# Moving weight sums and product splits from GpSimd to VectorE, their DMAs to ScalarE's queue, and decay differences to ScalarE

## The chip, the cores and the metric

One NeuronCore of one Trainium2 chip. The metric is device time in microseconds of one execution of the whole program. The engines are named PE (TensorE, with PEld for its weight loads), DVE (VectorE), ACT (ScalarE), POOL (GpSimd) and SP (SyncE, which here only issues DMAs). Each engine works through its own instructions in order.

## What is computed

Two residual layers over 272 tokens (16 learned meta tokens and 256 frames) of width 2048, all in float32. Layer 0 runs gated linear attention (GLA, 4 heads) beside stick-breaking attention (8 heads); layer 1 is a Mamba-2 mixer (SSD) with 8 groups of 8 heads.

```python
# layer 0
proj = einsum('btd,de->bte', h, w_in)
o_gla = rms_norm_groups(gla(gq, gk, gv, log_a)) * silu(gr)
o_sb  = stick_breaking(sq, sk, sv) * silu(sr)
h = layer_norm(alpha * h + einsum('bte,ed->btd', concat(o_gla, o_sb), w_out))
# layer 1
z, xbc, dt = split(einsum('btd,de->bte', h, w_in)); xbc = silu(conv(xbc))
a_cum = cumsum(dt * a_neg)
l_mat = exp(where(causal, a_cum[t] - a_cum[s], -inf))
y = einsum(l_mat * (C_t . B_s), x * dt) + d_skip * x        # per head
h = layer_norm(alpha * h + einsum('bte,ed->btd', rms_norm_groups(y * silu(z)), w_out))
```

The weights are drawn in float32, and the output is 256 x 2048.

## The kernel before

**Every product in three parts.** The matrix products are made from a high part and a low part of each operand: `three` issues high x high, high x low and low x high (L214 to L216). So each weight tile of 128 x 2048, a *unit*, is loaded on SP's queue (`load_unit`, L176) and split: ScalarE copies it to the rounded type (`whi`, L191), and VectorE subtracts that from the original (`wlo`, L192). `split` takes the engine of the subtraction as an argument. A unit's next-but-one is loaded when it starts, and the next is split while it is multiplied. The unit's 48 matmuls are issued in four quarters of 12.

**Side tasks.** Everything else is written as generators; `tick` advances each running one by one `yield`, once after every quarter of a unit. So a `yield` in a task is a distance of 12 matmuls in the order in which the program is written. The framework's planner then fixes each engine's order from that program order and a simulated timeline.

**Weight sums** (`quad_sums`, layer 0). The output product of layer 1 is made for six of its eight groups (`NS7`) with seven block products in place of eight, which needs sums of blocks of the output weights. For each of 6 groups and 2 column halves, two tiles of 128 x 2048 (four blocks of 512 columns, tile `quad`, one buffer) are loaded, four blocks are replaced by differences in four instructions (L573), and the tile is stored to DRAM (`qs`). These 24 blocks are made during layer 0. Loads (L569) and stores (L577) are on SP's queue, the differences on GpSimd. The steps of one block are 5 yields after the load, 4 differences with a yield each, 2 yields, the store, 2 yields.

**GLA and stick-breaking heads** (layer 0). `mix_gla` and `mix_sb` copy the scores from PSUM to `spad` (ScalarE, L828 and L931), mask them with three selects on GpSimd (`causal`, L288), split them (`parts_of`: ScalarE L680, VectorE L681) and multiply with the values (`values`, L739). TensorE's order has the values at a fixed place between matmuls of the units.

**Block products** (layer 1). `product_load` fetches 128 x 2 x 512 blocks (`praw`, L590), from the weights or from `qs`, on SP's queue; `product_split` splits them, with the subtraction of the 48 that come from `qs` on GpSimd and of the other 36 on VectorE; `product` makes six matmuls (L614) and adds the bank to the accumulator on VectorE (L619). Two loads run ahead.

**Decay** (`decay1`, layer 1). For a group, `load_decay` broadcasts 8 rows of cumulated decays to all partitions (tile `ebc`, one buffer, SP's queue, L1206). For each head VectorE makes min(ebc - est, 0) in two instructions (256 columns, L1239; 144 columns, L1240), `est` being a value per partition; ScalarE takes Exp of two heads at a time (L1242). Later VectorE multiplies with the masked scores `cb` (L1267, four instructions a group), and `mix_ssd` multiplies the result `M` on TensorE (L1424).

GpSimd also has, in layer 1, every third second half of the late units' splits (L192 with `raw`, 21 of them), the gate products and the sums of squares.

Of the kernel before, what the change touches and what calls it, by code (L numbers as in the profile page):

```python
# [8 lines left out]
AF = mybir.ActivationFunctionType  # L9
ALU = mybir.AluOpType  # L10
# [23 lines left out]
def _plan():  # L34
# [36 lines left out]
SEVEN = (  # L71
    ("a11", 0, False, 0, True, (0, 0)),
    ("a12", 3, False, 1, True, (0, 0)),
    ("s2", 2, True, 0, False, (1, 0)),
    ("s3", 1, True, 1, True, (1, 1)),
    ("s1", 0, True, 0, False, (1, 1)),
    ("n22", 3, True, 1, False, (1, 0)),
    ("s4", 2, False, 0, False, (0, 1)),
)
PRODUCTS = [(g, q, n) for g in range(NS7) for q in range(2) for n in range(7)]  # L80
# [19 lines left out]
def _wait(*tasks):  # L100
    for t in tasks:
        while not t.done:
            yield
# [14 lines left out]
class _Body:  # L118
# [440 lines left out]

    def quad_sums(self):  # L560

        nc, sub = self.nc, self.nc.gpsimd.tensor_tensor
        for g in range(NS7):
            for q in range(2):
                d = self.sums[g, q] = self.tc.dram_tile([2, P, 2048], F32, name=self.nm("qs"))
                for c in range(2):
                    b = self.lp.tile([P, 4, 512], F32, tag="quad", name=self.nm("quad"))
                    flat = b.rearrange("p a c -> p (a c)")
                    nc.sync.dma_start(flat, self.quad_rows(g, q)[c])  # L569
                    for _ in range(5):  # L570
                        yield
                    for o, x, y in ((0, 1, 0), (1, 2, 1), (2, 2, 0), (3, 2, 3)):
                        sub(b[:, o, :], b[:, x, :], b[:, y, :], op=ALU.subtract)  # L573
                        yield
                    for _ in range(2):
                        yield
                    nc.sync.dma_start(d[c], flat)  # L577
                    for _ in range(2):
                        yield

    def product_load(self, k):
# [10 lines left out]
    def product_split(self, k):  # L592
        if k >= len(PRODUCTS):
            return
        is_sum = SEVEN[PRODUCTS[k][2]][2]
        raw = self.praw.pop(k).rearrange("p k c -> p (k c)")
        self.pparts[k] = self.split(raw, 1024, self.nc.gpsimd if is_sum else self.nc.vector)

    def product(self, k):

# [612 lines left out]
    def decay1(self, g):  # L1213
        nc, lp = self.nc, self.lp
        act, vec, mm = nc.scalar.activation, nc.vector, nc.tensor.matmul
        bc = self.cur["bc", g]
        self.silu1(bc, None if g else vec)
        yield
        if g:
            yield from _wait(*self.mixers[6 + g - 1])  # L1220
        else:
            yield from _wait(self.tasks["dt"], self.tasks["res"])
            self.load_decay(0)
            yield
            yield
        if g > 1:
            bch, bcl = [a for a in lp.tile([P, 2, T + S], F32R, tag="gz", name=self.nm("bcp")).rearrange("p a c -> a p c")]
            act(bch, bc, AF.Copy)
            vec.tensor_tensor(bcl, bc, bch.bitcast(F32), op=ALU.subtract)
            pairs = ((bch, bch), (bch, bcl), (bcl, bch))  # L1230
        else:
            pairs = ((bc, bc),)

        M = lp.tile([P, HPG, 400], F32, tag="M", name=self.nm("M"))
        self.cur["M", g] = M
        eb = self.cur["ebc", g]
        for h in range(HPG):
            gh = g * HPG + h
            vec.tensor_scalar(M[:, h, 0:256], eb[:, h, 0:256], self.est[:, 0, 0, gh : gh + 1], 0.0, op0=ALU.subtract, op1=ALU.min)  # L1239
            vec.tensor_scalar(M[:, h, 256:400], eb[:, h, 256:400], self.est[:, 0, 1, gh : gh + 1], 0.0, op0=ALU.subtract, op1=ALU.min)  # L1240
            if h % 2:
                act(M[:, h - 1 : h + 1, :], M[:, h - 1 : h + 1, :], AF.Exp)  # L1242
                yield
        mt = self.mt
        e2 = self.est2[:, 0, g * HPG : (g + 1) * HPG].rearrange("p (h o) -> p h o", o=1).broadcast_to([16, HPG, 16])
        vec.tensor_tensor(mt, eb[:16, :, 400:416], e2, op=ALU.subtract)
        vec.tensor_scalar(mt, mt, 0.0, None, op0=ALU.min)
        act(mt, mt, AF.Exp)
        yield

        for _ in range(2 if g else 0):
            yield
        zb = self.zbank()
        pin = self.tc.keep_in_program_order
        for o, s0, n, t0 in ((zb[:, 16:272], 0, P, 0), (zb[:, 272:416], P, P, 112), (zb[:16, 0:16], 2 * P, NM, 240)):
            for i, (b, c) in enumerate(pairs):
                pin(mm(o, b[:, s0 : s0 + n], c[:, T + t0 :], start=i == 0, stop=i == len(pairs) - 1))
        yield
        cb = lp.tile([P, 416], F32, tag="cb", name=self.nm("cb"))
        act(cb, zb[:, :416], AF.Copy)  # L1260
        self.causal(cb[:, 16:128], 112, False, 16)
        self.causal(cb[:, 272:400], 128, False)
        self.causal(cb[:16, 0:16], 16, False)
        yield
        for h in range(0, HPG, 2):
            c = cb[:, 16:416].rearrange("p (o c) -> p o c", o=1).broadcast_to([P, 2, 400])
            vec.tensor_tensor(M[:, h : h + 2, :], M[:, h : h + 2, :], c, op=ALU.mult)  # L1267
            yield
        c = cb[:16, 0:16].rearrange("p (o c) -> p o c", o=1).broadcast_to([16, 2, 16])
        m = mt.rearrange("s (p j i) t -> s j p i t", j=2, i=2)  # L1270
        for j in range(2):
            for p in range(2):
                vec.tensor_tensor(self.mt2[32 * j : 32 * j + 16, 2 * p : 2 * p + 2, j, :], m[:, j, p], c, op=ALU.mult)
        yield
# [391 lines left out]
```

## Time and profile before

| | |
|---|---|
| median of 3 runs | 1528.98 us (1519.80 to 1532.24) |
| the profiled execution | 1524.72 us, span 1522.9 us |
| TensorE busy | 1401.1 us (92%), 10559 matmuls |
| VectorE busy | 1183.1 us (78%) |
| ScalarE busy | 800.3 us (53%) |
| GpSimd busy | 556.3 us (37%) |
| mean granted TensorE clock | 0.960 |
| DMA | 325.96 MB, 214 GB/s |

Layer 0 runs to about 770 us of the span, layer 1 from about 800. In a row of the profile stand the line, the engine, the operation and the tiles written and read (out<-in); a wait names the releaser, and the clock is that granted to TensorE as a share of full speed. A mean length is one over instructions that may have been held up; the minimum or the median of a group shows what the same instruction takes undisturbed.

### The profile page before, as it was taken

How to read it: one execution, taken by the hardware profiler on the slowest of the kernel's cores; microseconds unless marked ns; L12 is line 12 of the kernel's file. 1: busy time of each engine (PE TensorE's matmuls, PEld its weight loads, DVE VectorE, ACT ScalarE, POOL GpSimd, SP SyncE). 2: the span in 40 equal slices, each digit the busy share in tenths (PEclk: the TensorE clock that was granted, in tenths of full speed). 3: DMA queues.
4: the chain of work that ended last, by engine and by line, in shares of the span. 5: the costliest groups of instructions: out<-in, count | busy, mean ns of one | idle time of the engine just before them, and what ended most of it. 6: DMA issues, size and time to landing. Idle time of an engine off the chain costs nothing.

```text
span 1522.9 us, 26579 instructions
## 1 busy us (share of the span) xinstructions
PE 1401.1 (92%) x10559; PEld 1340.8 (88%) x10559; DVE 1183.1 (78%) x1812; ACT 800.3 (53%) x1171; POOL 556.3 (37%) x413
## 2 busy tenths in 40 slices
PE   9899999799899999999949998797987988989998
PEld 8799999799898999999948987797987888889886
DVE  7869676587475664668886998789798987888977
ACT  6446354255254544546765656465564565645661
POOL 2253523433434100017001535454454463545331
PEclk9999999899899999999979999898998999989999
DMA  9878778687676555553445556565665565655551
GB/s 343 289 270 295 276 254 302 248 286 274 233 293 252 168 164 182 176 161 132 166 145 208 201 180 238 167 218 179 229 208 178 196 215 192 214 181 208 185 201 56
DMA packets 88252, 325.96 MB, mean 214 GB/s; under 512 B 27904, under 2 KB 30784, under 8 KB 56640
## 3 DMA queue, kind: packets, MB, share of 16 engines
q1 hardware_dynamic: 87408, 323.48, 60.5%
q8 instruction: 83, 1.36, 0.4%
q10 hardware_dynamic: 720, 0.79, 0.1%
q14 instruction: 41, 0.34, 0.1%
HBM read 293.33 MB, written 30.91 MB: 213 GB/s over the span
## 4 chain that ended last, share of the span: by engine, by line
PE 50%; DVE 18%; DMA 13%; issue 6%; POOL 6%; ACT 4%; SPq 1%; ACTq 0%; POOLq 0%; DVEq 0%
PE pj L214 14%; PE pj L216 14%; PE pj L215 14%; DVE wlo L192 4%; POOL quad L573 4%; DMA quad<-in_wts 4%; PE pj L614 3%; DMA praw<-qs 3%; ACT whi L191 2%; DVE M L1267 2%; DMA qs<-quad 2%; DMA vdr<-vt 2%; DVE M L1239 2%; DMA vt<-vdr 1%; PE po L739 1%
## 5 line engine op out<-in xcount | busy, mean ns | idle before, releaser
L214 PE MATMUL pj<-xhi,whi 128*128 128x272 f32 (+4 forms) x2560 | 742.2, 290 | 29.2 <-DVE xt L1184 12.3
L216 PE MATMUL pj<-xhi,wlo 128*128 128x272 f32 (+4 forms) x2560 | 737.7, 289 | 8.9 <-DVE wlo L192 8.9
L215 PE MATMUL pj<-xlo,whi 128*128 128x272 f32 (+4 forms) x2560 | 738.3, 289 | 0.0
L192 DVE TENSOR_TENSOR wlo<-raw,whi 128x1024 fp32r<-128x1024 f32 (+2 forms) x365 | 502.9, 1385 | 134.6 <-ACT whi L191 132.3
L191 ACT ACTIVATE whi<-raw 128x1024 fp32r<-128x1024 f32 (+2 forms) x386 | 395.9, 1033 | 270.6 <-PE pj L215 206.2
L214 PEld LDWEIGHTS pj<-xhi,whi 128*128 128x128 f32 x2560 | 489.9, 192 | 39.7 <-DVE xt L1184 13.5
L216 PEld LDWEIGHTS pj<-xhi,wlo 128*128 128x128 f32 x2560 | 490.2, 192 | 10.0 <-DVE wlo L192 9.8
L215 PEld LDWEIGHTS pj<-xlo,whi 128*128 128x128 f32 x2560 | 490.0, 191 | 3.5
L573 POOL TENSOR_TENSOR quad<-quad 128x512 f32<-128x512 f32 x96 | 154.1, 1605 | 256.0 <-DMA quad<-in_wts 222.2
L192 POOL TENSOR_TENSOR wlo<-praw,whi 128x1024 fp32r<-128x1024 f32 x48 | 125.8, 2623 | 125.5 <-ACT whi L191 112.7
L191 ACT ACTIVATE whi<-praw 128x1024 fp32r<-128x1024 f32 x84 | 88.4, 1053 | 89.1 <-PE pj L614 41.3
L216 PE MATMUL pj<-mixh,wlo 128*128 128x272 f32 x384 | 112.7, 294 | 0.0
L214 PE MATMUL pj<-mixh,whi 128*128 128x272 f32 x384 | 112.5, 294 | 0.0
L215 PE MATMUL pj<-mixl,whi 128*128 128x272 f32 x384 | 112.4, 293 | 0.0
L1195 POOL TENSOR_TENSOR gz<-gz,xcl 128x512 f32<-128x512 f32 x16 | 28.8, 1801 | 165.6 <-ACT xcl L1194 165.6
L215 PEld LDWEIGHTS pj<-mixl,whi 128*128 128x128 f32 x384 | 74.3, 193 | 0.2
L216 PEld LDWEIGHTS pj<-mixh,wlo 128*128 128x128 f32 x384 | 74.5, 194 | 0.0
L214 PEld LDWEIGHTS pj<-mixh,whi 128*128 128x128 f32 x384 | 74.1, 194 | 0.1
L192 POOL TENSOR_TENSOR wlo<-raw,whi 128x1024 fp32r<-128x1024 f32 x21 | 55.0, 2617 | 47.5 <-ACT whi L191 47.4
L614 PE MATMUL pj<-whi,ssh 128*128 128x512 f32 x96 | 41.5, 432 | 27.8 <-DVE acc L619 25.5
L619 DVE TENSOR_TENSOR acc<-acc,pj 128x512 f32<-128x512 f32 x84 | 56.8, 677 | 12.5 <-PE pj L614 12.2
L1192 ACT ACTIVATE xcl<-xcl 128x544 f32<-128x544 f32 (+2 forms) x40 | 25.5, 639 | 60.0 <-DVE xcl L1191 60.0
(397 smaller groups left out, 1920.1 us busy)
## 6 DMA issues: line engine op xcount, KB each, us to landing
raw<-in_wts SPq DMA_DIRECT2D x188, 1024.0 KB, 6.1
quad<-in_wts SPq DMA_DIRECT2D x24, 1024.0 KB, 6.0
qs<-quad SPq DMA_DIRECT2D x24, 1024.0 KB, 4.8
praw<-qs SPq DMA_DIRECT2D x48, 512.0 KB, 4.4
praw<-in_wts SPq DMA_DIRECT2D x36, 512.0 KB, 4.2
ebc<-edr SPq DMA_DIRECT2D x8, 1664.0 KB, 6.7
raw<-in_wts SPq DMA_DIRECT2D x9, 256.0 KB, 5.5
vdr<-vt SPq DMA_DIRECT2D x8, 256.0 KB, 4.5
```

Source lines behind the costliest of these rows:

```text
L191: self.nc.scalar.activation(hi, src, AF.Copy)
L192: eng.tensor_tensor(lo, src, hi.bitcast(F32), op=ALU.subtract)
L214: mm(ps, whi, xhi, start=first, stop=False)
L215: mm(ps, whi, xlo, start=False, stop=False)
L216: mm(ps, wlo, xhi, start=False, stop=last)
L573: sub(b[:, o, :], b[:, x, :], b[:, y, :], op=ALU.subtract)
L614: mm(ps, a[:, j, :], b[:, j, :], start=f, stop=(j == 1 and a is yl), skip_group_check=True)
L619: self.nc.vector.tensor_tensor(a, a, ps, op=ALU.add)
L1192: act(c, c, AF.Exp, scale=-1.0)
L1195: (eng or self.nc.gpsimd).tensor_tensor(v, v, c, op=ALU.mult)
L1239: vec.tensor_scalar(M[:, h, 0:256], eb[:, h, 0:256], self.est[:, 0, 0, gh : gh + 1], 0.0, op0=ALU.subtract, op1=ALU.min)
L1267: vec.tensor_tensor(M[:, h : h + 2, :], M[:, h : h + 2, :], c, op=ALU.mult)
```

## The change

Four edits. The weight sums' subtractions go from GpSimd to VectorE. Their loads and stores go from SP's queue to ScalarE's, and two more yields stand between a store and the next load. The subtraction of every product split is on VectorE. The decay differences are made on ScalarE: Relu(est - ebc) in place of min(ebc - est, 0), followed by Exp with scale -1.

```diff
     def quad_sums(self):
-        nc, sub = self.nc, self.nc.gpsimd.tensor_tensor
+        nc, sub = self.nc, self.nc.vector.tensor_tensor
...
-                    nc.sync.dma_start(flat, self.quad_rows(g, q)[c])
+                    nc.scalar.dma_start(flat, self.quad_rows(g, q)[c])
                     for _ in range(5):
                         yield
...
-                    nc.sync.dma_start(d[c], flat)
-                    for _ in range(2):
+                    nc.scalar.dma_start(d[c], flat)
+                    for _ in range(4):
                         yield
...
     def product_split(self, k):
-        is_sum = SEVEN[PRODUCTS[k][2]][2]
         raw = self.praw.pop(k).rearrange("p k c -> p (k c)")
-        self.pparts[k] = self.split(raw, 1024, self.nc.gpsimd if is_sum else self.nc.vector)
+        self.pparts[k] = self.split(raw, 1024)
...
-            vec.tensor_scalar(M[:, h, 0:256], eb[:, h, 0:256], self.est[:, 0, 0, gh : gh + 1], 0.0, op0=ALU.subtract, op1=ALU.min)
-            vec.tensor_scalar(M[:, h, 256:400], eb[:, h, 256:400], self.est[:, 0, 1, gh : gh + 1], 0.0, op0=ALU.subtract, op1=ALU.min)
+            for s, c in ((0, slice(0, 256)), (1, slice(256, 400))):
+                act(M[:, h, c], eb[:, h, c], AF.Relu, bias=self.est[:, 0, s, gh : gh + 1], scale=-1.0)
             if h % 2:
-                act(M[:, h - 1 : h + 1, :], M[:, h - 1 : h + 1, :], AF.Exp)
+                act(M[:, h - 1 : h + 1, :], M[:, h - 1 : h + 1, :], AF.Exp, scale=-1.0)
```

## The prediction

> **What bounds the kernel now.** I first read the stages as a table of busy time (columns: stretch and its length, then busy time and instructions of TensorE, its weight loads, VectorE, ScalarE and GpSimd, then granted clock, DMA share, GB/s).
>
> ```profile
> span 1522.9 us, 26579 instructions
> 15.00:500.00 485.00, 454.53 (x3592) 449.64 (x3590) 344.96 (x518) 223.62 (x320) 191.54 (x134) 0.96 0.76 276
> 500.00:770.00 270.00, 268.17 (x2159) 266.48 (x2157) 188.55 (x330) 150.61 (x255) 44.65 (x67) 1.00 0.48 162
> 800.00:1400.00 600.00, 543.61 (x3955) 504.64 (x3954) 511.74 (x704) 340.00 (x466) 277.68 (x174) 0.95 0.58 201
> ```
>
> TensorE is the bound: from 500 to 770 us it is never idle and nothing can be won there. What can be lost or won is its idle time and its slow clock: 30 us idle before 500 us, 56 us idle in the steady part of layer 1, where the clock of 0.95 costs up to another 0.05 x 600 = 30 us. VectorE is the second engine there, busy 85% of the time; ScalarE has 57%.
>
> Second, the waits (who waited for whom, total us, times, longest us), and the timeline at the largest idle stretch of layer 0 (start, length, engine, line).
>
> ```profile
> POOL quad L573 <- DMA quad<-in_wts: 222.2, 20, 24.3
> PE pj L614 <- DVE acc L619: 25.5, 11, 7.9
> ACT s0h L680 <- POOL spad L288: 23.6, 4, 9.6
> 278.27 0.53 ACT L828 ACTIVATE spad<-z 128x432 f32<-128x432 f32 x1 [4.05 <-PE z L825]
> 285.92 5.28 POOL L573 TENSOR_TENSOR quad<-quad 128x512 f32<-128x512 f32 x4 [11.72 <-DMA quad<-in_wts]
> 291.15 0.68 POOL L288 TENSOR_SCALAR_AFFINE_SELECT spad<-spad 128x128 f32<-128x128 f32 x3
> 292.48 0.59 PE L739 MATMUL po<-s0h,gvh 128*128 128x272 f32 x1 [8.49 <-ACT s0h L680]
> ```
>
> The scores of a GLA head are in `spad` at 278.8. GpSimd has only 0.68 us to do on them, the causal selects, but its next instruction in order is a weight-sum subtraction that waits for its DMA until 285.9. So the selects run at 291.15, and TensorE stands for 8.49 us. The next head's stop has the same shape:
>
> ```profile
> 399.44 1.26 POOL L573 TENSOR_TENSOR quad<-quad 128x512 f32<-128x512 f32 x1 [9.93 <-DMA quad<-in_wts]
> 400.66 0.68 POOL L288 TENSOR_SCALAR_AFFINE_SELECT spad<-spad 128x128 f32<-128x128 f32 x3
> 267.00:305.00 38.00, 29.12 (x209) 28.35 (x208) 21.76 (x31) 10.84 (x14) 17.04 (x15) 0.87 0.65 249
> 381.00:419.00 38.00, 31.42 (x219) 30.86 (x218) 18.94 (x30) 10.04 (x14) 17.74 (x14) 0.82 0.64 233
> ```
>
> In these two stretches TensorE is idle 8.9 and 6.6 us and then runs slow: 0.13 x 38 = 4.9 and 0.18 x 38 = 6.8 us at most. Together 27 us.
>
> Third, layer 1, at one of its largest stops:
>
> ```profile
> 953.38 10.68 DVE L1267 TENSOR_TENSOR M<-M,cb 128x800 f32<-128x800 f32 x4 [0.42 <-POOL cb L288]
> 953.46 2.40 POOL L192 TENSOR_TENSOR wlo<-raw,whi 128x1024 fp32r<-128x1024 f32 x1
> 955.83 4.67 POOL L192 TENSOR_TENSOR wlo<-praw,whi 128x1024 fp32r<-128x1024 f32 x2
> 964.59 0.69 DVE L619 TENSOR_TENSOR acc<-acc,pj 128x512 f32<-128x512 f32 x1
> 965.42 0.76 PE L614 MATMUL pj<-whi,ssh 128*128 128x512 f32 x1 [7.67 <-DVE acc L619]
> L1267 DVE TENSOR_TENSOR M<-M,cb 128x800 f32<-128x800 f32 x32 | 51.0, 1651 | 2.7 <-POOL cb L288 2.7
> L1267 DVE TENSOR_TENSOR M<-M,cb x32: 977/984/7976, 815.1 to 1436.5; 128x800 f32<-128x800 f32 x32
> ```
>
> The last two rows are the group (busy us, mean ns) and min/median/max of one. Four products of 0.98 us take 10.68 us, because one lasts 7.98 us: as long as GpSimd runs three splits without a pause (953.46 to 960.50). The accumulation L619 that frees the next product's bank stands behind them, and TensorE waits 7.67 us. VectorE is not only full here, it is held up by GpSimd.
>
> **The change part by part.** Rows for the prices (group rows: busy us, mean ns; tile rows: min/median/max ns):
>
> ```profile
> L573 POOL TENSOR_TENSOR quad<-quad 128x512 f32<-128x512 f32 x96 | 154.1, 1605 | 256.0 <-DMA quad<-in_wts 222.2 <-DMA vt<-vdr 28.5
> L573 POOL TENSOR_TENSOR quad<-quad x96: 1258/1359/2382, 27.1 to 483.0; 128x512 f32<-128x512 f32 x96
> L192 DVE TENSOR_TENSOR wlo<-raw,whi 128x512 fp32r<-128x512 f32 x9 | 6.1, 692 | 0.9 <-ACT whi L191 0.9
> L192 POOL TENSOR_TENSOR wlo<-praw,whi 128x1024 fp32r<-128x1024 f32 x45 | 117.6, 2616 | 119.6 <-ACT whi L191 106.7 <-PE pj L614 10.6 <-DVE wlo L192 2.2
> L192 DVE TENSOR_TENSOR wlo<-praw,whi x36: 1205/1222/1998, 787.7 to 1421.9; 128x1024 fp32r<-128x1024 f32 x36
> L192 DVE TENSOR_TENSOR wlo<-raw,whi 128x1024 fp32r<-128x1024 f32 x109 | 161.4, 1482 | 29.0 <-ACT whi L191 28.1 <-issue 0.4
> L1239 DVE TENSOR_SCALAR M<-ebc,est 128x256 f32<-128x256 f32 x52 | 34.8, 668 | 3.8 <-PE po L1424 3.8
> L1240 DVE TENSOR_SCALAR M<-ebc,est 128x144 f32<-128x144 f32 x52 | 26.1, 503 | 0.0
> L647 ACT ACTIVATE ga<-po,cpk 128x272 f32<-128x272 f32 x8 | 3.8, 480 | 4.7 <-PE po L646 4.7
> L1442 ACT ACTIVATE ys<-y 128x256 f32<-128x256 f32 x24 | 9.6, 402 | 0.0
> L191 ACT ACTIVATE whi<-praw 128x1024 fp32r<-128x1024 f32 x84 | 88.4, 1053 | 89.1 <-PE pj L614 41.3 <-DMA praw<-qs 26.4 <-PE pj L215 9.0
> ACT whi L191 <- PE pj L215: 215.2, 160, 3.2
> 0.84 1.36 ACTq L321 DMA_DIRECT2D raw<-in_wts  x3
> SPq L577 <- POOL quad L573: 99.8, 19, 9.9
> SPq L569 <- DMA qs<-quad: 60.6, 16, 8.1
> SPq L1206 <- DVE M L1240: 69.4, 6, 12.1
> quad<-in_wts SPq DMA_DIRECT2D x24, 1024.0 KB, 6.0
> qs<-quad SPq DMA_DIRECT2D x24, 1024.0 KB, 4.8
> ```
>
> *Weight sums (layer 0).* GpSimd loses 96 x 1.605 = 154 us. VectorE gains 96 x 0.692 = 66 us, in a layer where it is busy 71%. It gets some back: 96 times it no longer shares time with a subtraction. TensorE sees neither while the splits are made ahead, as they are: ScalarE's wait 215.2 us for TensorE to free their tiles, and VectorE's follow. The stall goes with the select that no longer stands behind a load: at 278.8 + 0.7 + 0.6 the data would be ready near 280, four us before TensorE stops. What is late next is the head's split on VectorE (L681), and before it any subtraction waiting for its load. The two stops are worth 27 us; I take **-22**, 5 us going to the crowded first 50 us, where VectorE takes four more subtractions per block.
>
> *Their DMAs.* 48 issues leave SP, which no longer stands 99.8 us for GpSimd's subtractions and 60.6 us for the store before it reloads; the weight loads behind them go out earlier, hidden already by two units of lead. On ScalarE a load now waits for the previous store, with the splits `whi` and the evacuations queued behind. A step of the side tasks is 12 matmuls; 3592 + 2159 matmuls in 755 us with the idle left out (722.7 us) are 0.126 us each, so a step is 1.51 us. From store to reload there are now 4 steps, 6.0 us, against a landing of 4.8; from load to first subtraction 5 steps, 7.5 us against 6.0. Both fit by the median, with one us to spare, so I take nothing; bounds below. A block is 15 steps instead of 13, 22.6 us, so the 24 blocks end near 27 + 24 x 22.6 = 570 us instead of 483, still far ahead of the first product's splits at 787.7. An issue on ScalarE's queue takes 1.36 / 3 = 0.45 us, 48 of them 22 us; ScalarE is busy 46% before 500 us, so its idle time hides them.
>
> *Splits of the products (layer 1).* GpSimd loses 117.6 us of its 277.7 in the 600 us (48 x 2.616 = 126 in all); VectorE gains 45 x 1.222 = 55 us. In place of 2.6 us a split takes 1.2, so it is ready sooner.
>
> *Decay differences.* VectorE loses 34.8 + 26.1 = 60.9 us in the same 600 us. No row has a Relu. Nearest is L647, an activation with a pointer bias: 480 ns at 272 elements; the slope from L1442 and L191 is (1053 - 402) / 768 = 0.85 ns per element, so 466 and 371 ns at 256 and 144. 104 instructions (52 pairs): 43.5 us; bounds 52 x (402 + 307) = 37 from the row without a bias, and 52 x (530 + 435) = 50 with twice L647's surplus over it. ScalarE goes from 57 to 64%: hidden, except that the 8 pairs of a group are one chain of 8 x 0.84 = 6.7 us, with four Exp and some splits of 1.05 between, 10 us or more. They took VectorE 8 x (0.668 + 0.503) = 9.4. The last of them frees `ebc`, for which the SP queue stands 69.4 us already, with product loads behind it. I put 2 us on each of six groups, **+12**, with 0 and +30 as bounds.
>
> *What VectorE gets back.* In the 600 us its splits L192 take 109 x (1.482 - 1.222) = 28 us over the undisturbed, the products L1267 some 19 (51.0 - 32 x 0.984). GpSimd's moved splits are 42% of its busy time (20 us in proportion), and as in the stop above they are the back-to-back ones, so up to all 47; I take 33. VectorE: 511.7 + 55 - 60.9 - 33 = 473 us, 39 less. Idle and slow clock of TensorE come to 86 us; VectorE ends most of these waits, so I count 39 us, and 8 of slow clock that shorter stops spare: **-47**. With ScalarE's +12, layer 1 gives **-35**. The far ends are -65 (all 47 us back, so 53 of VectorE's and 12 of clock, and ScalarE free) and -4 (20 us back, so 26 and the clock's 8 less 30 for ScalarE).
>
> The SBUF page of the Trainium skill (SBUF — State Buffer, section Who interferes with whom) says that the pair of ports which VectorE shares with GpSimd is an exclusive lock, the loser blocked for the whole instruction; the 7.98 us product agrees. By that rule nearly all 47 us would come back instead of 33. The page ScalarE: Activation LUTs (Rules for kernel authors) speaks against the change: relu belongs on VectorE. By its figures (280 ns + 0.833 ns per element) a pair would be an estimated 493 + 400 ns, 46 us in all, near the 43.5 from rows. The page also has relu in every table set, which no run here shows.
>
> **Sum:** 1524.72 us, the profiled execution (span 1522.9), - 22 - 35 = 1467.7. The median of the runs shown is 1528.98, 4.3 us more, within their spread (1519.80 to 1532.24); I say 1468. Differences under 1% (15 us) can't be told from none here.
>
> **Rivals.**
> 1. *The layers gain fully:* the waits vanish as the lock goes (-65 and -27): 1433. For it: VectorE's held-up time all falls beside GpSimd's runs. Against: at 473 us of work it is still the second bound. Chance 0.17.
> 2. *Layer 1 keeps its time:* ScalarE's Relu chain holds `ebc` and so the SP queue and the lock gives back only its share (-4), while layer 0 gains 22: 1499. For it: the 69.4 us of SP. Chance 0.17.
> 3. *Nothing by over 1%:* layer 0's stop moves to VectorE, where L681 stands behind a subtraction as the selects did, and layer 1 as in 2: 1521. Chance 0.07.
> 4. *Slower:* VectorE takes over the wait of GpSimd's queue for its loads. That was 222.2 us over 24 blocks, 9 us a block. VectorE is idle (485 - 345) / 24 = 5.8 us a block, 3.0 after its 2.8 us of new work, more by what GpSimd's leaving gives back; I take 4. Beyond that each us counts 24 times, with splits and evacuations queued behind the waiting subtraction and ScalarE's queue behind the store that waits for it. At 8 us a block: 24 x 4 = 96, less layer 1's 35: 1586. It decides from 5.5 us a block (24 x 1.5 = 36). Against it: GpSimd had little else to do, and its reload came only after SP had stood for the store; load, subtractions and store are now 6.0 + 2.8 + 4.8 = 13.6 us of a block of 22.6. Chance 0.09.
>
> **Numbers.** My forecast, 1445 to 1490, has 0.50. Faster by over 1%: 0.50 + 0.17 + 0.17 = 0.84; within: 0.07; slower: 0.09. The range, 1425 to 1515, takes in most of rivals 1 and 2 with some us on each side and leaves out 3 and 4 but for an edge.
>
> **What will show it.** Right: no stop of TensorE over 3 us at L739 before 500 us; clock 1.00 there; GpSimd busy about 556 - 154 - 126 = 276 us in all; products L1267 with a mean near 1.1 us; splits L192 near 1.28; VectorE about 475 us per 600 of layer 1. Wrong: VectorE waiting for quad loads over 5 us a block, ScalarE waiting at the stores with `whi` late, or SP standing longer at L1206 and TensorE waiting for product splits.

## The result, and the profile after

The changed kernel takes 1487.66 us (median of 4 runs, 1486.01 to 1491.09) against 1528.32 before (1519.80 to 1532.24): a ratio of 0.974, 95% interval 0.970 to 0.979, some 40 us less. The forecast was 1468, the range 1425 to 1515. The profiled execution took 1486.17 us, its span is 1484.5.

The same table of stages as before the change (stretch and length, then busy time and instructions of TensorE, its weight loads, VectorE, ScalarE, GpSimd, then granted clock, DMA share, GB/s):

```profile
span 1484.5 us, 26516 instructions
PE 1392.4 (94%) x10559; PEld 1333.7 (90%) x10559; DVE 1141.6 (77%) x1828; ACT 841.5 (57%) x1299; POOL 261.7 (18%) x269
15.00:500.00 485.00, 463.30 (x3655) 457.91 (x3655) 358.63 (x621) 224.75 (x329) 30.72 (x41) 0.97 0.78 277
267.00:305.00 38.00, 34.40 (x261) 33.41 (x261) 25.95 (x44) 11.82 (x14) 1.45 (x4) 0.96 0.68 249
381.00:419.00 38.00, 30.43 (x224) 29.59 (x223) 25.43 (x43) 10.64 (x15) 2.22 (x5) 0.87 0.70 252
800.00:1400.00 600.00, 566.37 (x4183) 527.75 (x4182) 497.10 (x692) 405.54 (x615) 162.56 (x137) 0.98 0.62 211
```

In 800 to 1400 us TensorE's idle time fell from 56.4 to 33.6 us and its clock rose from 0.95 to 0.98; 4183 matmuls ran in place of 3955. Before 500 us the idle time fell only from 30.5 to 21.7 us. The stretch at 284 us got better; the one at 390 us is as bad as it was.

The two layers can be timed apart. At the turn from layer 0 to layer 1 TensorE stands for 12.94 or 12.95 us in both kernels, and the transposes behind this stop mark the same point (timeline of TensorE, before and after; start, length, line):

```profile
781.11 0.84 PE L1169 MATMUL po<-ident,dt_scr 64*128 64x64 f32 x4 [12.94 <-DVE dt_scr L1160]
```
```profile
777.90 0.84 PE L1168 MATMUL po<-ident,dt_scr 64*128 64x64 f32 x4 [12.95 <-DVE dt_scr L1159]
```

From the mark to the end of the span it was 741.8 us and is 706.6: **layer 1 won 35.2 us. Layer 0 won 3.2**, where 22 were forecast. Both are of one profile each: the six kernels with this layer 1, five of them below, lie between 706.6 and 712.6, so some us of the 35 may belong to layer 0.

Part of layer 0's gain was lost in the first 15 us, where 44 matmuls ran in place of 82; an experiment below prices it. The other part is in the waits of the changed kernel (who waited for whom, total us, times, longest):

```profile
ACT whi L191 <- DVE quad L573: 31.4, 8, 6.0
DVE quad L573 <- DMA quad<-in_wts: 28.8, 15, 5.5
ACT whi L191 <- DMA qs<-quad: 27.7, 7, 5.2
PE z L820 <- DVE gk L795: 12.5, 3, 7.6
ACT spad L827 <- DMA qs<-quad: 12.3, 2, 6.2
ACT spad L827 <- DVE quad L573: 10.7, 1, 10.7
```

The fifth and the third row are reloads: the load of a block waits on ScalarE's queue until the store of the last block has landed, 40 us in all, with the split or evacuation named in the row behind it. The first and the last are stores that wait there for VectorE's subtraction, 42 us. At the head near 390 us these waits hold each other up (timeline, all engines, cut to the rows that matter):

```profile
387.53 0.33 ACTq L569 DMA_DIRECT2D quad<-in_wts  x1
387.91 2.95 ACT L191 ACTIVATE whi<-raw 128x1024 fp32r<-128x1024 f32 x3 [3.23 <-DMA qs<-quad]
...
396.87 0.69 DVE L573 TENSOR_TENSOR quad<-quad 128x512 f32<-128x512 f32 x1 [5.50 <-DMA quad<-in_wts]
397.48 0.43 DVE L795 TENSOR_TENSOR gk<-pj,ke 128x272 f32<-128x272 f32 x1
...
397.97 1.27 PE L820 MATMUL z<-gq,gk 128*128 128x272 f32 x2 [7.57 <-DVE gk L795]
...
401.61 0.53 ACT L827 ACTIVATE spad<-z 128x432 f32<-128x432 f32 x1 [10.74 <-DVE quad L573]
```

ScalarE stood 3.23 us for the last store before it could issue the load at 387.53. So the load is late, VectorE stands 5.50 us for it at 396.87, and the keys `gk` of the head, which need VectorE for 0.43 us, are behind it. TensorE stands 7.57 us. GpSimd's queue used to do this to the selects.

Line numbers from L595 on are one lower than before in the changed kernel (L1267 is L1266), and four or five higher in some of the experiments' kernels (the subtraction is L578 there).

### The profile page after: what moved, and what is told of

It is laid out like the page before. It is cut to its first block, busy times and chain, and to the rows that moved or that the text cites. A ratio compares the mean times of both kernels' runs of the same rounds, so it can differ in the third digit from the quotient of the medians.

```text
span 1484.5 us, 26516 instructions
## 1 busy us (share of the span) xinstructions
PE 1392.4 (94%) x10559; PEld 1333.7 (90%) x10559; DVE 1141.6 (77%) x1828; ACT 841.5 (57%) x1299; POOL 261.7 (18%) x269
## 4 chain that ended last, share of the span: by engine, by line
PE 69%; DVE 14%; DMA 9%; issue 4%; ACT 2%; POOL 1%; SPq 0%; ACTq 0%; DVEq 0%; POOLq 0%
PE pj L214 19%; PE pj L216 19%; PE pj L215 19%; PE pj L613 6%; DVE wlo L192 4%; DMA quad<-in_wts 3%; DMA qs<-quad 3%; DVE M L1266 2%; PE po L1423 1%; DMA raw<-in_wts 1%; DVE xt L1183 1%; DVE quad L573 1%; PE po L738 1%; DVE y L1372 1%; ACT whi L191 1%
## 5 line engine op out<-in xcount | busy, mean ns | idle before, releaser
L192 DVE TENSOR_TENSOR wlo<-raw,whi 128x1024 fp32r<-128x1024 f32 (+2 forms) x365 | 450.1, 1240 | 140.5 <-ACT whi L191 138.2
L192 DVE TENSOR_TENSOR wlo<-praw,whi 128x1024 fp32r<-128x1024 f32 x84 | 111.3, 1326 | 18.4 <-ACT whi L191 18.1
L573 DVE TENSOR_TENSOR quad<-quad 128x512 f32<-128x512 f32 x96 | 69.8, 727 | 35.4 <-DMA quad<-in_wts 28.8
L192 POOL TENSOR_TENSOR wlo<-raw,whi 128x1024 fp32r<-128x1024 f32 x21 | 56.0, 2665 | 156.1 <-ACT whi L191 133.8
L300 POOL TENSOR_TENSOR gr<-gr,gsc 128x1088 f32<-128x1088 f32 x6 | 15.5, 2576 | 335.1 <-ACT gsc L299 335.1
L1239 ACT ACTIVATE M<-ebc,est 128x256 f32<-128x256 f32 (+1 forms) x128 | 46.1, 448 | 18.6 <-PE po L1423 18.6
```

The source lines that it names most:

```text
L192: eng.tensor_tensor(lo, src, hi.bitcast(F32), op=ALU.subtract)
L300: mul(c, c, e, op=ALU.mult)
L1239: act(M[:, h, c], eb[:, h, c], AF.Relu, bias=self.est[:, 0, s, gh : gh + 1], scale=-1.0)
```

## The experiments

All times are medians, each ratio is against runs of the kernel before taken beside it (their medians were 1525 to 1528 us). "Turn" is the mark above in the run's own profile, "layer 1" its span less the mark. One profile's turn is uncertain by some us: in four kernels whose layer 0 is that of before (before itself, two parts alone and the idle subtractions below) it lies at 781.1, 786.0, 785.9 and 778.4, 782.9 on average.

| kernel | us | ratio (95%) | turn | layer 1 |
|---|---|---|---|---|
| before | 1528.32 | 1 | 781.1 | 741.8 |
| after | 1487.66 | 0.974 (0.970–0.979) | 777.9 | 706.6 |
| weight sums alone | 1523.05 | 0.997 (0.995–0.999) | 776.6 | 740.8 |
| splits alone | 1497.98 | 0.980 (0.978–0.983) | 786.0 | 709.8 |
| Relu alone | 1520.03 | 0.996 (0.994–0.998) | 785.9 | 733.9 |
| first load held | 1478.20 | 0.968 (0.966–0.971) | 763.8 | 710.5 |
| sums back on GpSimd | 1498.15 | 0.981 (0.979–0.984) | 785.7 | 712.6 |
| DMAs on SP | 1472.41 | 0.963 (0.962–0.965) | 761.1 | 708.9 |
| more lead | 1482.00 | 0.970 (0.968–0.972) | 770.4 | 709.9 |
| loads on SP | 1460.53 | 0.956 (0.953–0.959) | 749.6 | 710.0 |
| idle GpSimd work | 1559.30 | 1.021 (1.018–1.023) | 778.4 | 775.1 |
| no Relu | 1475.14 | 0.965 (0.962–0.969) | 763.8 | 712.6 |
| last splits moved | 1466.87 | 0.961 (0.958–0.964) | 760.1 | 705.6 |
| both best | 1455.45 | 0.954 (0.952–0.957) | 746.9 | 706.8 |

**The parts alone.** Each of three kernels is the one before with one part of the change: the weight sums with their DMAs, the splits, the Relu.

```diff
-        nc, sub = self.nc, self.nc.gpsimd.tensor_tensor
+        nc, sub = self.nc, self.nc.vector.tensor_tensor
...
-                    nc.sync.dma_start(flat, self.quad_rows(g, q)[c])
+                    nc.scalar.dma_start(flat, self.quad_rows(g, q)[c])
...
-                    nc.sync.dma_start(d[c], flat)
-                    for _ in range(2):
+                    nc.scalar.dma_start(d[c], flat)
+                    for _ in range(4):
```

> The kernel before with the weight sums' edits alone (subtractions on VectorE, their loads and stores from ScalarE's queue, two more yields). Layer 0 ended 3 us earlier in the changed kernel than before (the 160-matmul mark after the last layer-0 units at 757 against 760 us), so if the layers don't depend on each other the time is 3 us less: about 1525, ratio 0.998. The first load should again be issued near 5 us and VectorE should wait for it. Rival: the sums' move also relieves layer 1 by starting it in another order: over 8 us less.

```diff
-        self.pparts[k] = self.split(raw, 1024, self.nc.gpsimd if is_sum else self.nc.vector)
+        self.pparts[k] = self.split(raw, 1024)
```

> The kernel before with all product splits on VectorE and nothing else. If GpSimd's back-to-back splits holding VectorE up are what costs (theory), layer 1 gains although VectorE gets 55 us of instructions more: 15 to 25 us less, about 1508, and the mean of the L1267 products falls from 1.65 us to about 1.3. Rival: VectorE's amount of work is what counts; it rises by 11 us net, so the time is the same or up to 10 us more.

```diff
-            vec.tensor_scalar(M[:, h, 0:256], eb[:, h, 0:256], self.est[:, 0, 0, gh : gh + 1], 0.0, op0=ALU.subtract, op1=ALU.min)
...
+                act(M[:, h, c], eb[:, h, c], AF.Relu, bias=self.est[:, 0, s, gh : gh + 1], scale=-1.0)
...
+                act(M[:, h - 1 : h + 1, :], M[:, h - 1 : h + 1, :], AF.Exp, scale=-1.0)
```

> The kernel before with the decay differences as Relu on ScalarE and nothing else. VectorE loses 61 us of layer 1. Theory: 10 to 20 us less, about 1513, the rest held back since the SP queue waits for the last Relu before it reloads ebc. Rival (VectorE's amount of work is what counts): 35 us or more less, near 1490. Rival from the prediction: the Relu chain costs 12 us or more and the time does not fall.

Measured 1523, 1498 and 1520 us: -3, -28 and -6. The weight sums did as expected (their first load was issued at 5.1 us), the splits won more than the 15 to 25 us expected, and the Relu less than the 10 to 20. The splits carry most of the gain, and the weight sums almost none. What is odd is VectorE's load (stages of splits alone, then of Relu alone; columns as above, then VectorE's groups: busy us, mean ns):

```profile
800.00:1400.00 600.00, 560.59 (x4171) 525.56 (x4170) 525.46 (x802) 363.01 (x497) 176.67 (x133) 0.97 0.62 212
L1267 DVE TENSOR_TENSOR M<-M,cb 128x800 f32<-128x800 f32 x28 | 31.4, 1182 | 2.7 <-POOL cb L288 2.2 <-ACT xcl L1194 0.4
L1239 DVE TENSOR_SCALAR M<-ebc,est 128x256 f32<-128x256 f32 x60 | 24.6, 410 | 4.6 <-PE po L1424 4.4
```
```profile
800.00:1400.00 600.00, 551.44 (x4047) 511.48 (x4047) 464.30 (x606) 391.86 (x599) 278.82 (x176) 0.97 0.60 205
L1267 DVE TENSOR_TENSOR M<-M,cb 128x800 f32<-128x800 f32 x28 | 43.1, 1594 | 1.8 <-POOL cb L288 1.8
```

The version that gained 28 us has VectorE busy 525 us of 600, more than the 512 of before; the version in which VectorE fell to 464 us gained 6. The three stages do not hold the same work, though: counted for the 3955 matmuls of before, VectorE's 525 are 525.46 x 3955 / 4171 = 498 us, and its 464 are 454. So 13 us less on VectorE went with 28 us, and 58 us less with 6. How long VectorE is busy is therefore not by itself what TensorE waits for. With the splits off GpSimd the products took 1182 ns in place of 1746, and the first decay difference 410 in place of 668. With the Relu the products still took 1594. (The products of before in the same 600 us:)

```profile
L1267 DVE TENSOR_TENSOR M<-M,cb 128x800 f32<-128x800 f32 x28 | 47.2, 1746 | 2.3 <-POOL cb L288 2.3
```

**GpSimd's work put back, without its use.** The splits stay on VectorE, and GpSimd makes a subtraction of the same shape for each moved one. This is work in addition, into a tile that nobody reads:

```diff
+            self.nc.gpsimd.tensor_tensor(self.idle, self.pparts[k][0].bitcast(F32), self.idle, op=ALU.subtract)
```

> x2_splits_only (1498.0) with one more GpSimd instruction for each of the 48 moved splits: a 128x1024 subtraction of a spare tile from the rounded part, written to the spare tile, which nothing reads (in addition to the kernel's work, which is complete). So GpSimd is as busy as before the change and VectorE makes the splits. Theory (GpSimd's runs hold VectorE up): at least two thirds of the 28 us come back, 1515 or more, and L1267 has a mean over 1.5 us again. Rival (the split is ready sooner on VectorE, 1.2 against 2.6 us): the time stays within 6 us of 1498.

Measured 1559.30 us, 61 more than splits alone. Nobody waits for the idle tile by the trace, yet VectorE's instructions became longer (the tile's row, then the stage and VectorE's groups; the helper's lines are some five further on):

```profile
L602 POOL TENSOR_TENSOR idle<-whi,idle x48: 2343/2848/4150, 857.0 to 1439.7; 128x1024 f32<-128x1024 f32 x48
800.00:1400.00 600.00, 529.48 (x3732) 488.32 (x3732) 559.66 (x719) 324.68 (x441) 278.17 (x165) 0.94 0.56 190
L1272 DVE TENSOR_TENSOR M<-M,cb 128x800 f32<-128x800 f32 x28 | 49.2, 1812 | 1.0 <-POOL cb L288 1.0
L1244 DVE TENSOR_SCALAR M<-ebc,est 128x256 f32<-128x256 f32 x48 | 30.8, 641 | 2.5 <-PE po L1429 2.5
```

The products went from 1182 to 1812 ns, the decay difference from 410 to 641, and layer 1 from 709.8 to 775.1 us. GpSimd's own work coming late is no rival of this size: in layer 1 other engines wait for GpSimd 24 us in place of 21. Against the kernel before, GpSimd is as busy (278 us of the 600 in both), VectorE has the 48 splits more, and the time is 31 us longer. So what VectorE has to do counts too: the move costs about 31 us there and wins about 61 by sparing VectorE GpSimd's runs. That GpSimd runs beside VectorE costs more than the work that it takes off VectorE. In the Trainium skill this is the lock of the page SBUF — State Buffer, section Who interferes with whom; these lengths agree with it.

**Layer 0: the first load.** By the dependencies the first weight-sum load waits for nothing, and on ScalarE's queue it was placed at the very start (timeline of the changed kernel, then of the one before):

```profile
4.72 0.33 ACTq L569 DMA_DIRECT2D quad<-in_wts  x1
11.46 1.42 DVE L573 TENSOR_TENSOR quad<-quad 128x512 f32<-128x512 f32 x2 [3.31 <-DMA quad<-in_wts]
14.51 0.47 PE L215 MATMUL pj<-xlo,whi 128*128 128x272 f32 x1 [4.52 <-DVE xlo L370]
```
```profile
19.28 0.57 SPq L569 DMA_DIRECT2D quad<-in_wts  x1
```

VectorE stands 3.31 us for it while TensorE waits for VectorE's part of the first input. The next kernel holds this one load behind the last ScalarE instruction written so far:

```diff
+                    if (g, q, c) == (0, 0, 0):
+                        late = next(i for i in reversed(self.traced()) if i.engine == mybir.EngineType.Activation)
+                        with self.tc.issue_after(late):
+                            nc.scalar.dma_start(flat, self.quad_rows(g, q)[c])
```

> The changed kernel with the first weight-sum load queued on ScalarE behind the last of its instructions traced at that point, instead of at 4.7 us among the loads of the start. Theory: the start gets back the 4.5 us stop of TensorE near 10 us and the 7 us by which the unit stream was late at the 160-unit mark (86 against 79 us): about 1480, 7 us less than the changed kernel's 1487.7. Rival: what layer 0 lacks comes from VectorE's later waits for loads alone (the three stops ahead of the GLA scores); then within 2 us of 1487.7.

Measured 1478.20 us, 9.5 less; the load is issued at 36.3 us, the turn comes 14 us earlier. So this one load's place cost 10 to 14 us.

**Who makes the sums.** The same kernel with the subtractions back on GpSimd:

```diff
-        nc, sub = self.nc, self.nc.vector.tensor_tensor
+        nc, sub = self.nc, self.nc.gpsimd.tensor_tensor
```

> x4_first_held (1478.2) with the weight sums' subtractions back on GpSimd; their loads and stores stay on ScalarE's queue, four steps apart. Theory: the stop belongs to whichever engine queues its other work behind a late load, and GpSimd has the selects of the GLA scores there: TensorE's stops at the values come back (8.5 and 6.6 us before), those at the scores (5.0 us) go; about 1485. Rival: the loads, issued from ScalarE's queue and spaced wider, are in time for GpSimd, and VectorE has 66 us less to do: 1470 or less.

```profile
POOL quad L578 <- DMA quad<-in_wts: 223.5, 21, 41.2
```

Measured 1498.15 us, above both figures: 20 more than with VectorE. GpSimd stands 223.5 us for loads again, with the selects behind, and the turn is 21.9 us later. So with the first load out of the way, taking the subtractions off GpSimd is worth about the 22 us of the forecast.

**The queues.** The changed kernel with both DMAs on SP, and, with the first pair of lines only, the loads on SP and the stores on ScalarE:

```diff
-                    nc.scalar.dma_start(flat, self.quad_rows(g, q)[c])
+                    nc.sync.dma_start(flat, self.quad_rows(g, q)[c])
...
-                    nc.scalar.dma_start(d[c], flat)
+                    nc.sync.dma_start(d[c], flat)
```

> The changed kernel (1487.7) with the weight sums' loads and stores back on SP's queue; subtractions on VectorE and four steps as changed. On SP the first load stands behind the loads of the start by itself, so the start is as in x4_first_held. Theory: ScalarE's queue costs little apart from that first load, so the time is that of x4_first_held within 5 us, 1474 to 1483. Rival 1: ScalarE's waits at stores and reloads (27.7 us for stores to land, 31.4 us for subtractions) cost time: below 1472. Rival 2: SP standing for the subtractions makes the weight loads late: above 1485.

> The changed kernel with only the weight sums' loads back on SP's queue and the stores left on ScalarE's. Theory: the loads are what hurts (the first one at 4.7 us, and the reload that makes ScalarE wait for the store to land): within 4 us of x6_dma_sp, 1469 to 1476. Rival: the stores hurt as much, since ScalarE waits at them for VectorE's subtractions (31.4 us): 1478 to 1485.

Measured 1472.41 and 1460.53 us; the turns are 16.8 and 28.3 us earlier than in the changed kernel. The first lies between the theory's figure and the rival's, the second well under both. Their waits (both DMAs on SP, then loads alone):

```profile
DVE quad L573 <- DMA quad<-in_wts: 48.1, 19, 6.1
SPq L569 <- DMA qs<-quad: 64.7, 21, 8.5
SPq L577 <- DVE quad L573: 36.1, 13, 6.8
```
```profile
DVE quad L573 <- DMA quad<-in_wts: 26.3, 14, 3.5
ACT whi L191 <- DVE quad L573: 9.8, 4, 3.7
SPq L569 <- DMA qs<-quad: 54.1, 20, 8.1
15.00:500.00 485.00, 478.29 (x3848) 473.37 (x3847) 376.82 (x653) 240.25 (x349) 36.97 (x47) 1.00 0.80 288
```

Most of the 16.8 us by which the turn is earlier with both on SP is the first load again, which SP issues at 18.7 us: holding that load alone moved the turn by 14.1. What is left for the queue is 1478.20 less 1472.41, some 6 us (2.7 by the turns), just outside the 5 that my theory allowed. All of ScalarE's waits at `quad` are gone then, while VectorE waits longer for loads (48.1 against 25.7 us with the first load held). By this comparison ScalarE's waits cost more than VectorE's.

The stores alone are the other way round: on ScalarE's queue in place of SP's, with the loads on SP in both kernels, they made it 12 us faster. With the loads alone on SP the wait for the store is nearly as long, 54.1 us, and stands on a queue that computes nothing; SP is spared the 36.1 us for stores; ScalarE waits only 9.8 us at them; and VectorE's wait for loads falls from 48.1 to 26.3 us. Which of these waits the 12 us belong to wasn't tried. TensorE is idle 6.7 us before 500, at a clock of 1.00.

**More lead.** The version with the first load held, with 8 steps from load to subtraction in place of 5, and 1 and 3 in place of 2 and 4 around the store:

```diff
-                    for _ in range(5):
+                    for _ in range(8):
...
-                    for _ in range(2):
-                        yield
+                    yield
...
-                    for _ in range(4):
+                    for _ in range(3):
```

> x4_first_held with 8 steps instead of 5 between a weight-sum load and its first subtraction, one less ahead of the store and one less behind it (16 steps a block). Theory: what is left of layer 0's stops is VectorE standing at a load (25.7 us in x4_first_held) with the GLA keys behind it; these waits fall below 10 us, TensorE's stop of 5.0 us at the scores goes: about 1471. Rival: the stops come from the chain store, reload, landing as a whole, and moving the steps only moves the wait to ScalarE: 1476 to 1482.

```profile
ACT whi L191 <- DMA qs<-quad: 43.7, 11, 5.6
DVE quad L578 <- DMA quad<-in_wts: 25.5, 12, 3.5
```

Measured 1482.00 us, a little more than the 1478.20 that it starts from (the intervals of the ratios overlap). My theory fell: VectorE waits for the loads as before (25.5 us; 25.7 with 5 steps), and ScalarE's wait for the store grew from 23.3 to 43.7. The lead was taken from the store's side, and the wait went there.

**What is left in layer 1.** On the kernel with both DMAs on SP: the decay differences back on VectorE, or the last 21 GpSimd splits moved to VectorE:

```diff
-                act(M[:, h, c], eb[:, h, c], AF.Relu, bias=self.est[:, 0, s, gh : gh + 1], scale=-1.0)
+            vec.tensor_scalar(M[:, h, 0:256], eb[:, h, 0:256], self.est[:, 0, 0, gh : gh + 1], 0.0, op0=ALU.subtract, op1=ALU.min)
...
```

> x6_dma_sp with the decay differences back on VectorE (min of the difference in place of Relu). Alone the Relu gave 6 us while VectorE lost 47 us of busy time; if VectorE's amount of work counts little, undoing it costs 3 to 9 us, about 1478. Rival: with the splits on VectorE it has less room, and the Relu is worth 20 us or more here: above 1490.

```diff
-            eng = self.nc.gpsimd if pool else self.nc.vector
+            eng = self.nc.vector
```

> x6_dma_sp (1472.4) with the last 21 splits of GpSimd, the second halves of late units, on VectorE too. By the same reasoning as for the 48 (28 us for 48, VectorE 55 us more of instructions against 45 to 57 us less held up): 25 us held up beside them against 26 us of new instructions, so 5 to 12 us less, about 1464. Rival: VectorE is now near enough to the bound (495 us of 600) that the added work counts: 1473 to 1480.

Measured 1475.14 and 1466.87 us against 1472.41. The last splits give 5.5 us and the Relu 3, but the intervals overlap in both cases, so neither is settled. Layer 1 by the profiles has the same signs: 705.6 and 712.6 us against 708.9. What the last splits do to VectorE is plain (its products from 800 to 1400 us with both DMAs on SP, then with the last splits moved):

```profile
L1266 DVE TENSOR_TENSOR M<-M,cb 128x800 f32<-128x800 f32 x29 | 34.9, 1259 | 1.4 <-POOL cb L288 1.4
L1266 DVE TENSOR_TENSOR M<-M,cb 128x800 f32<-128x800 f32 x29 | 26.8, 984 | 0.6 <-POOL cb L288 0.6
```

With no split left on GpSimd the mean product takes 984 ns, the median of the undisturbed ones before.

**Both best.** Loads on SP and the last splits moved, together:

```diff
-                    nc.scalar.dma_start(flat, self.quad_rows(g, q)[c])
+                    nc.sync.dma_start(flat, self.quad_rows(g, q)[c])
...
-            eng = self.nc.gpsimd if pool else self.nc.vector
+            eng = self.nc.vector
```

> x11_load_sp (1460.5) with the last 21 splits of GpSimd on VectorE too, which gave 5.5 us on x6_dma_sp: if the two parts, one in layer 0 and one in layer 1, don't depend on each other, 1455, and 1451 to 1460 by what one run tells from another. Rival: the earlier start of layer 1 takes the gain away: 1460 or more.

Measured 1455.45 us (1454.50 to 1461.77), ratio 0.954: 4.6% under the kernel before, 32 us under the changed one. It is the fastest of all, though its interval overlaps that of loads on SP.

## Why the prediction was right, and where it was not

**The bounds** held: TensorE sets the time, and what is won is its idle time and slow clock.

**Weight sums.** The select's stall left as said: at L738 TensorE lost 1.1 us in all of layer 0, where one stop alone had taken 8.49. But before 500 us the clock was 0.97 and not 1.00, and a stop of 7.57 us stood at the scores instead. Two terms failed. One is the start: "the crowded first 50 us" had 5 us, for the subtractions, and that a load without dependencies would go out at 4.7 us was not foreseen; its place cost 10 to 14. The other is the step *Their DMAs*, "Both fit by the median, with one us to spare, so I take nothing". They did not fit (DMA issues of the changed kernel: count, KB, median us to landing; the tile's row: ns of the issue, then first and last start):

```profile
quad<-in_wts ACTq DMA_DIRECT2D x24, 1024.0 KB, 6.4
qs<-quad ACTq DMA_DIRECT2D x24, 1024.0 KB, 6.2
L569 ACTq DMA_DIRECT2D quad<-in_wts x24: 334/334/335, 4.7 to 464.1; - x24
```

The store landed in 6.2 us in place of 4.8, over the 6.0 that I had counted between store and reload. And the blocks did not last 22.6 us each: from the first load to the last it is (464.1 - 4.7) / 23 = 20.0 us, so 15 steps took 1.33 us each and not 1.51, and the four before the reload 5.3. There was no slack, and late landings stood on the queue of the engine that makes the splits. With the first load held the store landed in 5.0 us, but the blocks were shorter still, (462.2 - 63.7) / 22 = 18.1 us, so four steps took 4.8 and the wait stayed. Moving both DMAs back to SP is worth 17 us in layer 0, moving the loads alone 28, of which the first load's place is 14; for the rest, 3 and 14 us, I had said nothing. This is rival 4's mechanism on a small scale: VectorE waits 28.8 / 24 = 1.2 us a block, far from the 5.5 at which it decides.

**Layer 1** came out near the -35 forecast, but by luck, and not for the reason given. The splits L192 take 1278 ns, as said, and VectorE's load was foreseen well: 497.1 us for 4183 matmuls are 470 for the 3955 of before, against 473. The failing step is the next one, "VectorE ends most of these waits, so I count 39 us". By it the splits alone would have made the kernel slower by 22, as VectorE would gain 55 and get 33 back, and the Relu alone faster by 49, that is 61 less 12. Measured were -28 and -6. One term under it was too small: with the splits alone VectorE's busy time fell by 13 us for equal work, so it got 55 + 13 = 68 us back, not 33. But the step itself fails too, as 13 us of VectorE's time were worth 28 and the Relu's 58 only 6. What the idle work shows is that sparing VectorE GpSimd's runs wins more than the added splits cost; that it is the length of the single hold-up, like the product of 7.98 us, which decides fits but was only argued. Also, *What VectorE gets back* left out the decay differences themselves: 410 against 668 ns in 52 instructions are 13 us which the splits' move gives back and which I had counted as Relu's gain. The edits thus share a gain, and two wrong terms made a right sum.

**Decay differences.** The rows of the Relu and of the products in the changed kernel (busy us, mean ns), and ScalarE's table load:

```profile
L1239 ACT ACTIVATE M<-ebc,est 128x256 f32<-128x256 f32 x64 | 31.7, 495 | 18.6 <-PE po L1423 18.6
L1239 ACT ACTIVATE M<-ebc,est 128x144 f32<-128x144 f32 x64 | 25.6, 400 | 0.0
L1266 DVE TENSOR_TENSOR M<-M,cb 128x800 f32<-128x800 f32 x32 | 41.0, 1338 | 1.7 <-POOL cb L288 1.7
L262 ACT ACT_TABLE_LOAD x1 | 1.3, 1283 | 0.8 <-PEq L1654 0.8
SPq L1205 <- ACT ysq L1438: 45.6, 6, 9.3
```

495 and 400 ns in place of 466 and 371: inside the bounds. The +12 for ScalarE's chain doesn't show: SP waits for `ebc` 45.6 us in place of 69.4 (the row names `ysq`, which stands right behind the last Relu in ScalarE's order). The products' mean is 1338 ns, not "near 1.1 us", since 21 splits are still on GpSimd: with those moved it is 1020. GpSimd's 262 us are near the 276 said.

The page ScalarE: Activation LUTs of the Trainium skill (Rules for kernel authors) puts relu on VectorE. Here the Relu on ScalarE gained 6 us alone, and 3 us, within the uncertainty, once the product splits were off GpSimd: in neither case did it cost time. Whether its worth lies in VectorE's being held up isn't shown. That relu is in every table set, as the same page of the Trainium skill has it (Table sets: the hidden batching unit), agrees with the single table load that this kernel has.

**The rivals.** Rivals 2 and 3 expected layer 1 to keep its time: it didn't. Rival 1's full gain of 92 us was reached by no version; with the loads on SP and the last splits moved, 70 of it were.

## What to carry to other kernels

Price a move between VectorE and GpSimd by how far the one holds the other up (compare the mean with the minimum of the same instruction), not by VectorE's busy time; here more instructions on VectorE made the kernel faster. When you compare busy times of a stretch, count them for the same work. For a DMA that waits for a landing or for another engine, look at what stands behind it in its queue: here the reloads were better on SP, and the stores, which wait for VectorE, on ScalarE's queue. Look also at where a DMA without dependencies ends up. Test the parts of a change alone, as a right total can hide wrong terms, and take one cause at a time: two moves of the same DMAs had the first load in common.

## What the runs showed of the hardware

What GpSimd's runs cost beside VectorE is larger than I had put it: 48 subtractions of 2.85 us on GpSimd, which nobody reads, cost 61 us of the kernel's time, and lengthened even the small decay differences from 410 to 641 ns. With no split left on GpSimd the products of the 600 us took 984 ns in the mean, where they had taken 1746.

A store's landing does not go by the queue that issues it in this kernel. Its median was 4.8 us from SP before and 6.2 with both DMAs on ScalarE's queue, but 5.0 on the same queue with the first load held, 5.1 with the stores alone there, and 5.7 with both back on SP. What sets it wasn't tried.
